# The state space model's two tables of powers, multiplied out on GpSimd instead of VectorE

## The chip, the core and the metric

The kernel runs on one core of a Trainium2 chip. The core has a matrix engine (TensorE, in the profile PE, with its weight loads as PEld), VectorE (DVE), ScalarE (ACT), GpSimd (POOL) and SyncE (SP), which issues most DMAs. Each engine works through its own queue of instructions in order; semaphores tie the queues together. The metric is the device time of one execution in microseconds; lower is better.

## What is computed

Three transformer-like blocks on 512 positions of width 1024, in float32. The first block mixes positions by four branches that are gated and merged: a linear-attention recurrence, a spatial gating unit, a short convolution and a diagonal state space model (S5). A feed-forward layer follows, then two attention layers with convolved feed-forward layers. The change touches the S5 branch:

```python
def s5_mixer(u, a_re, a_im, b_re, b_im, c_re, c_im, d, log_dt, glu_w):
    ...
    bb_re = q_re[..., None] * b_re - q_im[..., None] * b_im
    bb_im = q_re[..., None] * b_im + q_im[..., None] * b_re
    bu_re = jnp.einsum('gnc,bsgc->bsgn', bb_re, ug)
    bu_im = jnp.einsum('gnc,bsgc->bsgn', bb_im, ug)
    ...
    _, _, x_re, x_im = lax.associative_scan(_complex_affine_combine, (ar, ai, bu_re, bu_im), axis=1)
    y = (jnp.einsum('gcn,bsgn->bsgc', c_re, x_re) - jnp.einsum('gcn,bsgn->bsgc', c_im, x_im))
```

## The kernel before

Matrix products run in a split precision: `wload` (L142) fetches a weight tile of 128x1024 by a DMA on SP into `raw` (4 buffers), ScalarE rounds it to `whi` (L152) and VectorE subtracts to get `wlo` (L153, both 3 buffers); `mm3` (L169) then multiplies three times, hi by hi, hi by lo and lo by hi. So each weight tile costs VectorE one subtraction of 128x1024, and a matmul that reads `wlo` waits for it.

`_first_block` (L1165) writes its branches in this order: projections of the recurrence (`_rwkv`), the small parameters of S5 (`_s5_setup`, L950), the convolution (`_conv_branch`, products `cg` and `cy`), the spatial gating (`_sg_branch`, L878), the merge of the convolution (`_merge`, tiles `gp` and `yp`), the shift of the recurrence (`_rwkv_shift`, with dot products on VectorE, L328), the tables of S5 (`_s5_tables`, L1003) and its branch (`_s5_branch`). The program's scheduler doesn't keep this order. It takes for each engine the ready instruction that was written first, by its own idea of durations, and so fills gaps of one branch with instructions of a later one. The queue of each engine is fixed when the kernel is built.

In the gating, four value tiles `svp` are multiplied on TensorE, pass a GELU (`gelu2`, L243), are normalised on VectorE (`sgz`, L909 to L917) and go back to TensorE as weights of `sgm` (L928).

S5 works on chunks of eight positions. Its tables are two complex arrays of 128x(8 groups x 8 powers x 16 channels): Q holds powers 0 to 7 of the transition times the input matrix `bb`, W2 holds powers 1 to 8 times the output matrix `c4`. `_cmul` (L939) makes each from six operations of 128x1024, two for each of the four products and sums that make up the real and the imaginary part:

```python
    V.tensor_tensor(ore, are, bre, OP.mult)
    V.tensor_tensor(t, aim, bim, OP.mult)
    V.tensor_tensor(ore, ore, t, add)
    V.tensor_tensor(oim, aim, bre, OP.mult)
    V.tensor_tensor(t, are, bim, OP.mult)
    V.tensor_tensor(oim, oim, t, OP.subtract if conj else OP.add)
```

In the profile these are L942 to L947 with the tiles `s_Q`, `s_W` and the temporary `s_tq`; L1017 changes the sign of the imaginary part of W2. TensorE transposes Q (`s5q`, L1031) and multiplies it with `cb`, the output matrix (`s5k`, L1037, 32 small matmuls). ScalarE copies that product to `s_kt`; a DMA of POOL's queue takes it to a scratch in HBM, twelve more bring it back spread out as `s_ti` (L1048), and VectorE copies it into the Toeplitz tiles `s_toe` (L1051). `s5y` (L1138, L1141) multiplies W2 and `s_toe` near the end of the branch. Beside these, VectorE makes a table of rotations `s_ph` by doubling (L1056 to L1076, again by `_cmul`, on small tiles).

Of the kernel before, what the change touches and what calls it, by code (L numbers as in the profile page):

```python
# [18 lines left out]
OP = mybir.AluOpType  # L19
# [919 lines left out]
def _cmul(V, ore, oim, are, aim, bre, bim, t, conj=False):  # L939

    add, sub = (OP.add, OP.subtract) if conj else (OP.subtract, OP.add)
# [6 lines that stand above are left out]
# [55 lines left out]
def _s5_tables(K, sp, z):  # L1003
    nc, V = K.nc, K.nc.vector
    pr, pi, bb, c4, mag, sn, cs, s = (z[n] for n in ("pr", "pi", "bb", "c4", "mag", "sn", "cs", "s"))
    t8 = lambda n: sp.tile([128, 8], F32, name=n)

    Q = [K.g(f"s5_Q{x}", "e4", shape=(128, 8, 128)) for x in range(2)]
    W2 = [K.g(f"s5_W{x}", "e4", shape=(128, 8, 128)) for x in range(2)]
    tq = K.g("s5_tq", "e4", shape=(128, 8, 128))  # L1010
    v4 = lambda z: z.rearrange("p g (k c) -> p g k c", k=8)
    w = [128, 8, 8, 16]
    pk = lambda z, o: z[:, :, o:o + 8].unsqueeze(3).to_broadcast(w)
    mk = lambda z: z.unsqueeze(2).to_broadcast(w)
    _cmul(V, v4(Q[0]), v4(Q[1]), pk(pr, 0), pk(pi, 0), mk(bb[:, 0]), mk(bb[:, 1]), v4(tq))
    _cmul(V, v4(W2[0]), v4(W2[1]), pk(pr, 1), pk(pi, 1), mk(c4[:, 0]), mk(c4[:, 1]), v4(tq))
    V.tensor_scalar(W2[1], W2[1], -1.0, None, OP.mult)  # L1017

    cb = K.g("s5_cb", "e", shape=(128, 2, 8, 32))
    nc.gpsimd.memset(cb, 0.0)  # L1020
    for h in range(2):
        hs = slice(h * 64, (h + 1) * 64)
        V.tensor_copy(cb[hs, 0, :, h * 16:(h + 1) * 16], c4[hs, 0])
        V.tensor_scalar(cb[hs, 1, :, h * 16:(h + 1) * 16], c4[hs, 1], -1.0, None, OP.mult)

    QT = [K.g(f"s5_QT{x}", "e4", shape=(128, 8, 128)) for x in range(2)]
    for x in range(2):
        for q4 in range(2):
            ps = K.sm("s5q")
            for p in range(4):  # L1030
                nc.tensor.transpose(ps[:, p * 128:(p + 1) * 128], Q[x][:, 4 * q4 + p], K.ident)  # L1031
            nc.scalar.copy(QT[x][:, 4 * q4:4 * q4 + 4].rearrange("p a b -> p (a b)"), ps)

    ps = K.sm("s5k")
    for p in range(8):
        for x in range(2):
            nc.tensor.matmul(ps[:, p * 32:(p + 1) * 32], lhsT=Q[x][:, p], rhs=cb[:, x, p], start=x == 0, stop=x == 1)  # L1037
    kt = sp.tile([128, 256], F32, name="s5_kt")
    nc.scalar.copy(kt, ps[:, 0:256])
    scr = K.scratch.tile([128, 256], F32, name="s5_scr")  # L1040
    nc.gpsimd.dma_start(scr, kt)
    ti = [K.g(f"s5_ti{x}", "e4", shape=(128, 4, 256)) for x in range(2)]
    toe = [K.g(f"s5_toe{x}", "e4", shape=(128, 8, 128)) for x in range(2)]
    for x in range(2):
        nc.gpsimd.memset(ti[x], 0.0)
        for j in range(4 * x + 4):
            i0, o = max(j - 4 * x, 0), (7 - j) * 16
            nc.gpsimd.dma_start(ti[x][o:o + 16, i0:4],  # L1048
                                scr.rearrange("(k c) f -> c k f", c=16)[:, 4 * x + i0 - j:4 * x + 4 - j])
        for y in range(2):  # L1050
            V.tensor_copy(toe[y].rearrange("p g (i c) -> p g i c", i=8)[:, :, 4 * x:4 * x + 4],  # L1051
                          ti[x][:, :, y * 128:(y + 1) * 128].rearrange("p i (g c) -> p g i c", g=8))

    t2 = t8("s5_t2")
    for _ in range(3):
        V.tensor_tensor(mag, mag, mag, OP.mult)  # L1056
        V.tensor_tensor(t2, sn, cs, OP.mult)
        V.tensor_tensor(s, sn, sn, OP.mult)
        V.tensor_scalar(sn, t2, 2.0, None, OP.mult)
        V.tensor_scalar(cs, s, -2.0, 1.0, OP.mult, OP.add)  # L1060
    ph = [K.g(f"s5_ph{x}", "e", shape=(128, 8, 64)) for x in range(2)]
    tp = sp.tile([128, 8, 32], F32, name="s5_tp")
    V.memset(ph[0][:, :, 0:1], 1.0)
    V.memset(ph[1][:, :, 0:1], 0.0)
    V.tensor_copy(ph[0][:, :, 1], cs)
    V.tensor_copy(ph[1][:, :, 1], sn)
    n = 1
    while n < 63:
        m = min(n, 63 - n)
        last = lambda z: ph[z][:, :, n:n + 1].to_broadcast([128, 8, m])  # L1070
        _cmul(V, ph[0][:, :, n + 1:n + m + 1], ph[1][:, :, n + 1:n + m + 1], ph[0][:, :, 1:m + 1],
              ph[1][:, :, 1:m + 1], last(0), last(1), tp[:, :, 0:m])
        n += m
    rr = K.g("s5_rr", "e", shape=(128, 8, 64))
    V.tensor_copy(rr, mag.unsqueeze(2).to_broadcast([128, 8, 64]))
    V.memset(rr[:, :, 0:1], 0.0)  # L1076
    return dict(W2=W2, toe=toe, QT=QT, ph=ph, rr=rr)
# [87 lines left out]
def _first_block(K):  # L1165
    nc, d = K.nc, K.dram
    with ExitStack() as mix:
# [5 lines left out]
        with K.tags(e=9, e4=8):  # L1173
            with K.tc.tile_pool(name="s5", bufs=1) as sp:
                x, g1, rs = _start(K)
                tiles = _rwkv(K, x, g1, rs)
                last = K.last
                with K.tc.issue_after(K.split_1):
                    z = _s5_setup(K, sp)
                yc = _conv_branch(K)  # L1180
                yb = _sg_branch(K, last)
                acc = [K.g(f"acc{m}", "xr") for m in range(8)]
                for _ in _merge(K, 2, yc, acc, ada):
                    pass
                la, pairs = _rwkv_shift(K, tiles, rs)
                with K.tc.issue_after(last):
                    tab = _s5_tables(K, sp, z)
            yd = _s5_branch(K, tab)
# [482 lines left out]
```

## Time and profile before

| | |
|---|---|
| Median of three runs | 2148.33 us (2146.29 to 2150.67) |
| Profiled execution | 2149.2 us |
| Its span, first to last instruction | 2147.4 us |
| PE, PEld busy | 98%, 79% |
| DVE busy | 66% |
| ACT busy | 43% |
| POOL busy | 1% |
| Granted clock of TensorE, mean | 0.992 |

The rows below come from one profiled execution. A busy share is of the whole span. In a timeline a row gives the start, the busy time, the engine, the line, the operation with its output and inputs, the shapes and the count; idle time before it and what ended it stand in brackets. Successive operations of one engine overlap, so they start closer together than their busy time. The granted clock is the share of its full rate (2.4 GHz) that TensorE was given; half of it is 1.2 GHz.

### The profile page before, as it was taken

The page shows a single profiled execution, that of the slowest core. Times are in us where ns is not written, and L with a number is a line of the kernel's source. Part 1 is how long each engine was busy: PE and PEld are TensorE (multiplying, and loading weights), DVE is VectorE, ACT ScalarE, POOL GpSimd, SP SyncE. Part 2 cuts the span into 40 slices and gives each one's busy share as a digit, 9 for nine tenths or more (in the row PEclk, how much of TensorE's full clock was granted, in tenths as well). Part 3 has the DMA queues.
Part 4 walks back from the last instruction along what each step waited for, and adds up shares of the span by engine and source line. Part 5 has one row for each costly group of instructions (what it writes and reads, how often), then busy time and mean ns, then how long its engine had stood idle before and what let it go on. Part 6 is the DMA issues. An engine that isn't in the chain of part 4 may idle for free.

```text
span 2147.4 us, 29518 instructions
## 1 busy us (share of the span) xinstructions
PE 2094.6 (98%) x11502; PEld 1692.7 (79%) x11502; DVE 1416.1 (66%) x2655; ACT 934.1 (43%) x1549; POOL 23.5 (1%) x44
## 2 busy tenths in 40 slices
PE   6999999999999999999999999999999999999998
PEld 4877787888888888897778888888887778788887
DVE  7997884755734344558876756747568867575775
ACT  3334432333523232446764423324469944243433
POOL 0010000000000000000000000000000000000000
PEclk9999999999999999999999999999999999999999
DMA  8355441123322232232212222232321122323222
GB/s 329 106 182 180 159 148 50 60 84 133 108 98 89 98 98 89 99 119 89 80 50 98 98 93 94 89 98 81 128 79 40 60 79 86 101 83 105 97 81 67
DMA packets 68091, 220.47 MB, mean 103 GB/s; under 512 B 8068, under 2 KB 11060, under 8 KB 67952
## 3 DMA queue, kind: packets, MB, share of 16 engines
q1 hardware_dynamic: 64704, 210.19, 29.6%
q0 software_dynamic: 2096, 6.30, 1.0%
q8 instruction: 91, 1.49, 0.3%
q10 hardware_dynamic: 1152, 2.10, 0.3%
q14 instruction: 48, 0.39, 0.1%
HBM read 215.25 MB, written 3.30 MB: 102 GB/s over the span
## 4 chain that ended last, share of the span: by engine, by line
PE 85%; DVE 6%; ACT 4%; DMA 2%; issue 1%; DVEq 0%; ACTq 0%; SPq 0%
PE mm L174 62%; PE gp L174 7%; PE vt L174 3%; PE yp L174 2%; DMA raw<-ada_w 2%; PE pT L1336 1%; DVE wlo L153 1%; PE po L1349 1%; PE fin L174 1%; PE s L1316 1%; PE s L1317 1%; ACT whi L152 1%; DVE raw L328 1%; ACT p L1324 1%; PE pmt L643 1%
## 5 line engine op out<-in xcount | busy, mean ns | idle before, releaser
L174 PE MATMUL mm<-hi,whi 128*128 128x512 f32 x2088 | 829.7, 398 | 19.1 <-ACT hi L161 17.8
L174 PE MATMUL mm<-hi,wlo 128*128 128x512 f32 x2088 | 830.5, 398 | 1.1 <-DVE wlo L153 1.1
L174 PE MATMUL mm<-lo,whi 128*128 128x512 f32 x2088 | 829.2, 397 | 1.1 <-DVE lo L165 0.5
L152 ACT ACTIVATE whi<-raw 128x1024 fp32r<-128x1024 f32 (+3 forms) x341 | 350.3, 1030 | 754.9 <-PE mm L174 600.9
L153 DVE TENSOR_TENSOR wlo<-raw,whi 128x1024 fp32r<-128x1024 f32 (+3 forms) x341 | 403.5, 1186 | 180.2 <-ACT whi L152 170.7
L174 PEld LDWEIGHTS mm<-hi,whi 128*128 128x128 f32 x2088 | 395.7, 190 | 110.3 <-ACT hi L161 20.8
L174 PEld LDWEIGHTS mm<-lo,whi 128*128 128x128 f32 x2088 | 394.9, 189 | 91.1 <-DVE lo L165 2.7
L174 PEld LDWEIGHTS mm<-hi,wlo 128*128 128x128 f32 x2088 | 394.7, 189 | 89.9 <-DVE wlo L153 2.0
L1521 DVE TENSOR_TENSOR u<-mm,spr 128x512 f32<-128x512 f32 x88 | 60.6, 688 | 82.5 <-PE mm L174 82.2
L174 PE MATMUL gp<-hi,wlo 128*128 128x512 f32 x256 | 102.7, 401 | 3.3 <-DVE wlo L153 3.3
L174 PE MATMUL gp<-hi,whi 128*128 128x512 f32 x256 | 104.1, 407 | 0.9 <-ACT whi L152 0.9
L174 PE MATMUL gp<-lo,whi 128*128 128x512 f32 x256 | 102.9, 402 | 0.0
L1541 DVE TENSOR_TENSOR x<-x,mm 128x512 f32<-128x512 f32 x48 | 33.0, 687 | 96.1 <-PE mm L174 96.1
L1240 DVE SCALAR_TENSOR_TENSOR x<-mm,modv,x 128x512 f32<-128x512 f32 x32 | 24.0, 751 | 91.0 <-PE mm L174 91.0
L1522 ACT ACTIVATE cv<-u,vecs 128x512 f32<-128x512 f32 x88 | 71.3, 810 | 3.4 <-DVE u L1521 3.2
L1524 DVE SCALAR_TENSOR_TENSOR cv<-u,vecs,cv 128x510 f32<-128x510 f32 x88 | 66.0, 750 | 3.1
L1523 DVE SCALAR_TENSOR_TENSOR cv<-u,vecs,cv 128x511 f32<-128x511 f32 x88 | 65.6, 746 | 2.3 <-ACT cv L1522 2.1
L1532 ACT ACTIVATE cth<-cv 128x512 f32<-128x512 f32 x44 | 27.8, 632 | 86.2 <-DVE cv L1524 86.2
L174 PEld LDWEIGHTS gp<-hi,wlo 128*128 128x128 f32 x256 | 48.4, 189 | 15.6 <-DVE wlo L153 5.1
L1324 ACT ACTIVATE p<-p,at_m 128x128 f32<-128x128 f32 (+1 forms) x96 | 53.4, 557 | 14.7 <-DVE at_m L1323 13.7
L174 PEld LDWEIGHTS gp<-hi,whi 128*128 128x128 f32 x256 | 48.6, 190 | 13.4 <-ACT whi L152 1.8
L174 PEld LDWEIGHTS gp<-lo,whi 128*128 128x128 f32 x256 | 48.6, 190 | 10.6 <-issue 0.4
(532 smaller groups left out, 2612.1 us busy)
## 6 DMA issues: line engine op xcount, KB each, us to landing
raw<-w_up SPq DMA_DIRECT2D x88, 512.0 KB, 3.3
raw<-ffn_w SPq DMA_DIRECT2D x64, 512.0 KB, 3.3
raw<-w_in SPq DMA_DIRECT2D x49, 512.0 KB, 3.4
raw<-ada_w SPq DMA_DIRECT2D x32, 512.0 KB, 3.9
raw<-w_down SPq DMA_DIRECT2D x32, 384.0 KB, 3.1
ada_w<-ada_w SPq DMA_DIRECT2D x16, 512.0 KB, 8.7
raw<-w_out SPq DMA_DIRECT2D x16, 512.0 KB, 3.4
raw<-w_down SPq DMA_DIRECT2D x16, 512.0 KB, 3.3
```

Of the source, the lines that this page charges most:

```text
L152: nc.scalar.activation(hi[:, :n], raw[:, :n], AF.Copy)
L153: nc.vector.tensor_tensor(lo[:, :n], raw[:, :n], hi[:, :n].bitcast(F32), OP.subtract)
L174: self.nc.tensor.matmul(out, lhsT=a, rhs=b, start=first and n == 0, stop=last and n == total - 1)
L328: K.nc.vector.tensor_tensor_reduce(raw, raw, row, scale, 0.0, OP.mult, OP.add, out)
L1240: V.scalar_tensor_tensor(K.xr[m], ps, K.modv[:, 40 + m:41 + m], K.xr[m], OP.mult, OP.add)
L1324: A.activation(p[:, 0:n], p[:, 0:n], AF.Exp, bias=nm, scale=-1.0, accum_out=l)
L1521: V.tensor_tensor(u, ps, rs, OP.mult)
L1522: A.activation(c, u, AF.Identity, bias=K.vec("conv_b_2", l * 44 + j), scale=tap(2))
L1523: V.scalar_tensor_tensor(c[:, 1:], u[:, 0:S - 1], tap(1), c[:, 1:], OP.mult, OP.add)
L1524: V.scalar_tensor_tensor(c[:, 2:], u[:, 0:S - 2], tap(0), c[:, 2:], OP.mult, OP.add)
L1532: A.activation(th, gt, AF.Tanh, scale=0.5)
L1541: V.tensor_tensor(K.xr[m], K.xr[m], ps, OP.add)
```

## The change

The two complex products that make Q and W2, and the sign change of W2, are issued on GpSimd in place of VectorE. The operations, their operands and the tiles are the same.

```diff
     pk = lambda z, o: z[:, :, o:o + 8].unsqueeze(3).to_broadcast(w)
     mk = lambda z: z.unsqueeze(2).to_broadcast(w)
-    _cmul(V, v4(Q[0]), v4(Q[1]), pk(pr, 0), pk(pi, 0), mk(bb[:, 0]), mk(bb[:, 1]), v4(tq))
-    _cmul(V, v4(W2[0]), v4(W2[1]), pk(pr, 1), pk(pi, 1), mk(c4[:, 0]), mk(c4[:, 1]), v4(tq))
-    V.tensor_scalar(W2[1], W2[1], -1.0, None, OP.mult)
+    G = nc.gpsimd
+    _cmul(G, v4(Q[0]), v4(Q[1]), pk(pr, 0), pk(pi, 0), mk(bb[:, 0]), mk(bb[:, 1]), v4(tq))
+    _cmul(G, v4(W2[0]), v4(W2[1]), pk(pr, 1), pk(pi, 1), mk(c4[:, 0]), mk(c4[:, 1]), v4(tq))
+    G.tensor_scalar(W2[1], W2[1], -1.0, None, OP.mult)
```

Lines behind the diff are one higher in the changed kernel (L1037 becomes L1038). The scheduler makes other queues of it, up to the middle of the recurrence; from there on all queues are the same.

VectorE's queue, where the first table product stood; the numbers in the names tell buffers apart (`wlo_889` is the split that the first `svp` reads). Before:

```order
L870 SCALAR_TENSOR_TENSOR cy_789<-cg_659,vecs_69,cy_789 128x510
L942 TENSOR_TENSOR s5_Q0_1674<-s5_pw_609,s5_bb_651 128x1024
L943 TENSOR_TENSOR s5_tq_1678<-s5_pw_609,s5_bb_651 128x1024
L863 TENSOR_TENSOR cg_724<-mm_763,cg_724 128x512
L153 TENSOR_TENSOR wlo_889<-raw_887,whi_888 128x1024
L870 SCALAR_TENSOR_TENSOR cy_829<-cg_724,vecs_69,cy_829 128x511
L944 TENSOR_TENSOR s5_Q0_1674<-s5_Q0_1674,s5_tq_1678 128x1024
```

The same place in the changed kernel, the last rows ahead of `wlo_889`:

```order
L1077 MEMSET s5_rr_1826 128x8
L1060 TENSOR_SCALAR s5_sn_539<-s5_t2_1767 128x8
L1061 TENSOR_SCALAR s5_xr_540<-s5_s_636 128x8
L1067 COPY s5_ph1_1784<-s5_sn_539 128x8
L1066 COPY s5_ph0_1783<-s5_xr_540 128x8
L863 TENSOR_TENSOR cg_724<-mm_763,cg_724 128x512
L942 TENSOR_TENSOR s5_ph0_1783<-s5_ph0_1783 128x8
L943 TENSOR_TENSOR s5_tp_1785<-s5_ph1_1784 128x8
L153 TENSOR_TENSOR wlo_889<-raw_887,whi_888 128x1024
L870 SCALAR_TENSOR_TENSOR cy_829<-cg_724,vecs_69,cy_829 128x511
```

The table products are gone from the queue, and the small operations of the rotation tables, 18 of them (beside `cg`) up to `wlo_889`, have come forward.

POOL's queue in the changed kernel, from the memset of `cb` on (before, the memset of `ti0` came next):

```order
L1021 MEMSET s5_cb_1692 128x512
L942 ISA
L942 TENSOR_TENSOR s5_Q0_1674<-s5_pw_609,s5_bb_651 128x1024
L943 TENSOR_TENSOR s5_tq_1678<-s5_pw_609,s5_bb_651 128x1024
L945 TENSOR_TENSOR s5_Q1_1675<-s5_pw_609,s5_bb_651 128x1024
L944 TENSOR_TENSOR s5_Q0_1674<-s5_Q0_1674,s5_tq_1678 128x1024
L942 TENSOR_TENSOR s5_W0_1676<-s5_pw_609,s5_bc_533 128x1024
L946 TENSOR_TENSOR s5_tq_1678<-s5_pw_609,s5_bb_651 128x1024
L945 TENSOR_TENSOR s5_W1_1677<-s5_pw_609,s5_bc_533 128x1024
L947 TENSOR_TENSOR s5_Q1_1675<-s5_Q1_1675,s5_tq_1678 128x1024
```

Q0 is complete with the fourth product and Q1 with the eighth. The other four products, the sign change, the memset of `ti0` and the DMAs of `kt` and `ti` follow.

TensorE's queue at the `s5k` of the tables and the `sgm` of the gating. Before:

```order
L1037 MATMUL s5k<-s_cb,s_Q_1674 128x32
L1037 MATMUL s5k<-s_cb,s_Q_1675 128x32
L928 MATMUL sgm<-sg_wsT,sgz 64x128 x4
L174 MATMUL mm<-hi,whi 128x512
L174 MATMUL mm<-lo,whi 128x512
```

And now:

```order
L1038 MATMUL s5k<-s_cb,s_Q_1675 128x32
L1038 MATMUL s5k<-s_cb,s_Q_1674 128x32
L928 MATMUL sgm<-sg_wsT,sgz 64x128 x2
L174 MATMUL mm<-hi,whi 128x512
L928 MATMUL sgm<-sg_wsT,sgz 64x128 x2
L174 MATMUL mm<-lo,whi 128x512
```

Before, all 32 `s5k` stood ahead of `sgm`; now 19 do, and of the other 13 the last four stand ahead of the S5 projection.

## Rows read from the trace of the kernel before

**Rows 1.** The page's first part: TensorE's busy time, its share, instructions.

```profile
PE 2094.6 (98%) x11502; PEld 1692.7 (79%) x11502; DVE 1416.1 (66%) x2655; ACT 934.1 (43%) x1549; POOL 23.5 (1%) x44
```

**Rows 2.** Busy time of each engine by stretch.

```profile
core 0: us, PE busy (x) PEld busy (x) DVE busy (x) ACT busy (x) POOL busy (x), PEclk, DMA share, GB/s
85.00:119.60 34.60, 34.60 (x206) 30.48 (x205) 34.10 (x63) 13.81 (x25) 0.00 (x0) 1.00 0.34 115
125.00:130.00 5.00, 1.57 (x12) 1.32 (x12) 5.00 (x19) 0.37 (x1) 0.76 (x2) 0.50 0.48 167
```

**Rows 3.** Timeline of TensorE, 100 to 137 us.

```profile
100.81 0.28 PE L174 MATMUL svp<-wlo,hi 128*128 128x256 f32 x1
...
119.57 2.18 PE L1031 MATMUL s5q<-k_ident,s_Q 128*128 128x128 f32 x16
121.66 4.12 PE L1037 MATMUL s5k<-s_cb,s_Q 128*128 128x32 f32 x32
129.21 1.12 PE L928 MATMUL sgm<-sg_wsT,sgz 128*64 128x128 f32 x8 [3.43 <-DVE sgz L917]
...
136.22 0.39 PE L174 MATMUL mm<-hi,whi 128*128 128x512 f32 x1
```

**Rows 4.** Timeline of VectorE, 88 to 130 us.

```profile
88.11 0.28 DVE L947 TENSOR_TENSOR s_bb<-s_bb,s_tb 128x128 f32<-128x128 f32 x1
...
88.97 1.22 DVE L942 TENSOR_TENSOR s_Q<-s_pw,s_bb 128x1024 f32<-128x1024 f32 x1
90.10 1.22 DVE L943 TENSOR_TENSOR s_tq<-s_pw,s_bb 128x1024 f32<-128x1024 f32 x1
91.24 0.68 DVE L863 TENSOR_TENSOR cg<-mm,cg 128x512 f32<-128x512 f32 x1
91.84 1.22 DVE L153 TENSOR_TENSOR wlo<-raw,whi 128x1024 fp32r<-128x1024 f32 x1
...
113.14 0.42 DVE L909 BATCH_NORM_STATS2 bn_s<-sgz 128x6 f32<-128x256 f32 x1
...
126.29 1.21 DVE L947 TENSOR_TENSOR s_W<-s_W,s_tq 128x1024 f32<-128x1024 f32 x1
...
129.48 0.68 DVE L1017 TENSOR_SCALAR s_W<-s_W 128x1024 f32<-128x1024 f32 x1
```

**Rows 5.** Timelines of VectorE and TensorE around the wait at 171 us.

```profile
154.51 0.42 DVE L1051 COPY s_toe<-s_ti 128x512 f32<-128x512 f32 x1
...
169.94 1.22 DVE L153 TENSOR_TENSOR wlo<-raw,whi 128x1024 fp32r<-128x1024 f32 x1
...
171.21 0.50 PE L174 MATMUL gp<-hi,wlo 128*128 128x512 f32 x1 [2.05 <-DVE wlo L153]
...
173.19 0.63 PE L174 MATMUL gp<-hi,whi 128*128 128x512 f32 x1
```

**Rows 6.** Timeline of VectorE: the last of the rotation tables' operations.

```profile
173.40 0.42 DVE L947 TENSOR_TENSOR s_ph<-s_ph,s_tp 128x248 f32<-128x248 f32 x1
```

**Rows 7.** Timeline of POOL.

```profile
54.14 0.96 POOL L1045 MEMSET s_ti<- 128x1024 f32 x1 [50.61 <-DVE modv L328]
...
129.78 2.26 POOL L1048 DMA_DIRECT2D s_ti<-s_scr  x4 [2.75 <-DMA s_scr<-s_kt]
132.04 0.97 POOL L1045 MEMSET s_ti<- 128x1024 f32 x1
133.30 4.13 POOL L1048 DMA_DIRECT2D s_ti<-s_scr  x8 [0.29 <-POOL s_ti L1045]
```

**Rows 8.** Timeline of VectorE beside the two memsets of POOL.

```profile
54.69 2.07 DVE L407 SCALAR_TENSOR_TENSOR x<-x,g,spr 128x512 f32<-128x512 f32 x3
...
131.71 1.33 DVE L1059 TENSOR_SCALAR s_sn<-s_t 128x8 f32<-128x8 f32 x1
```

**Rows 9.** Timelines of ScalarE and TensorE: the S5 projection's copy, the Toeplitz tiles' reader.

```profile
206.09 0.57 ACT L1085 COPY s5u<-mm 128x512 f32<-128x512 f32 x1
...
232.47 0.56 PE L1141 MATMUL s5y<-s_ub,s_toe 128*128 128x64 f32 x4
```

## The prediction

> **What bounds the kernel now.** The page's first part says that TensorE is busy for 98% of the span [rows 1], so work on another engine costs time only where TensorE waits for it. The stretch table comes next. Between 85 and 119.6 us TensorE never pauses, but VectorE is busy for 34.10 of 34.60 us; right behind, TensorE works for 1.57 us of five, at a granted clock of 0.50, which is 1.2 of its 2.4 GHz [rows 2]. The timeline of TensorE shows why. It does the transposes `s5q` (119.57) and the products `s5k` (from 121.66), both read from the table Q, and then idles 3.43 us before `sgm` at 129.21, released by VectorE's normalised `sgz` (L917). At 136.22 matmuls are back at 0.39 us [rows 3]. So for some 6.7 us after the wait it ran at half clock, which costs about half of that, 3.3 us: **6.7 us** for the wait and its clock. VectorE was late because its queue was full: the twelve table products, from 88.97 us on, stand among the weight splits (`wlo`) and the gating arithmetic [rows 4]. A second wait of 2.05 us, on a `wlo` at 169.94, comes from the same full queue; seven matmuls behind it take 0.63 in place of 0.39 us, 1.7 us more [rows 5]. Together **10.4 us** of TensorE's time hang on VectorE's queue between 89 and 171 us.
>
> **The change, part by part.**
>
> *Removed from VectorE.* Twelve products start 1.13 us apart (88.97 to 90.10), 13.6 us; the sign change of W2[1] holds the queue for about 0.6 (busy 0.68) [rows 4]: 14.2 us. The four `toe` copies leave the stretch too, as their input now comes later: 4 x 0.42 = 1.7 busy [rows 5], some 1.4 by start to start. The last two small products of the phase table come in ahead of the wait at 171 (0.7). VectorE's queue up to 171 us is **14.9 us** shorter.
>
> *Moved on VectorE.* 52 small operations of the rotation tables (`s_ph`, `s_rr` and their sources) stand ahead of the gating arithmetic now instead of between 130 and 173.4 us. The last and longest is busy for 0.42 us [rows 6], most for 0.2 and overlapping: some 7 us, and no new work. But 18 of them, beside `cg`, now precede the `wlo` of 91.84 that the first `svp` needs at 100.81; it had ended by 93.06, so that split has 7.7 us of cover [rows 3, 4].
>
> *Added on POOL.* Thirteen instructions of 128x1024. No two-input operation of POOL is in this trace. The nearest row is its memset of the same size: 0.96 us for one stream [rows 7]. A product reads two streams and writes one. Side by side they give 0.96, one after another 2.88; I take two, **1.92 us**, since the write can overlap the reads. Twelve of those and 0.96 for the sign change are **24.0 us** (12.5 to 35.5). POOL can start when the table `s_bb` is done, 88.4 us [rows 4]. The transposes need Q1, the eighth product: 88.4 + 8 x 1.92 = 103.8, at the dear end 111.4, both ahead of 119.57 [rows 3]. If POOL runs freely, Q is in time, with at least 8 us of cover. By the Trainium skill (GPSIMD Engine Reference, section 3.1), which gives 4497 ns for 2048 elements, one product would be an estimated 2.25 us and POOL's work about 28 us.
>
> *Who else waits on POOL.* Behind the tables in POOL's queue stand the memset of `ti`, the DMA of `kt` and twelve of `ti`. They wait for `s5k` anyway, of which 13 of 32 now stand behind `sgm`, the last four just ahead of the projection whose copy `s5u` starts at 206.09 [rows 9]. From there: 2.75 us for the DMA of `kt`, 6.4 to issue the twelve others, 1 for the memset [rows 7], so about 214 with landing. The reader is `s5y` at 232.47 [rows 9]: hidden, with 18 us of cover. W2 is read by the same `s5y`. SP swaps a few neighbouring loads; TensorE gets no new work. I cost these at nothing.
>
> *Do the two engines run side by side?* This decides the sign. When POOL's memset ran at 132.04, a VectorE operation on 128x8 elements took 1.33 us from 131.71 and ended as the memset did; at 54.14 three operations with two inputs passed beside another memset undisturbed, 0.69 us each [rows 7, 8]. So the engines do hold each other off, for a whole instruction, but not in every combination. The pair that matters, two SBUF inputs on VectorE against a POOL instruction that reads, is not in this trace. Nothing lost is one bound; the other is all of POOL's 24.0 us, less what VectorE can do meanwhile with one input or one in PSUM: three operations of 0.68 (`cg` and two `cy`) and two of 0.42 (`bn_stats`), 2.9 us [rows 4]. That is 21.1 us. I take the upper end, since the row that shows a hold shows a full one, and most of VectorE's work here has two inputs in SBUF. The Trainium skill (SBUF — State Buffer, section "Who interferes with whom") says just this of that pair, an exclusive lock for the whole instruction, and that a GpSimd instruction that only writes spares two-input ones. Both memset rows agree with it; no row here shows the reading pair.
>
> *The sum.* VectorE's queue at 171 us: -14.9 + 21.1 = +6.2 us. TensorE waits for it there as before, and the waits move forward: the first is at `svp` (100.81), where the 18 small operations ahead of its split face POOL's, and the clock falls again there instead of at 129. The wait at `sgm` goes, but what is late next is the `wlo` stream. The profiled execution took 2149.2 us, 0.87 above the median of the runs, 2148.33. So 2149.2 + 6.2 = 2155.4, and against the median **2154.5 us**.
>
> **The rivals.**
>
> *Side by side, so faster.* The two engines barely hold each other, and VectorE's queue is 14.9 us shorter. TensorE reaches `sgm` after 19 of the 32 `s5k` at about 124 [rows 3]; VectorE, which before came to `sgz` behind all twelve products, is done by then. This gives back 6.7 us, with the wait at 171 up to 10.4: 2141.6 to 2137.9, say 2140. For it: DMA issues of POOL beside VectorE's work, and the pass at 54 us. Against: the hold at 131.71. It decides where VectorE loses less than 14.9 us, that is, under some six tenths of POOL's work.
>
> *POOL is the one held off, so no change.* If VectorE's back-to-back queue keeps the port, POOL advances only in its gaps. Up to 119.57 VectorE is freed of eleven products, all but that at 126.29 [rows 4], 12.4 us, takes in about 7 of small table work, and has 2.9 that hold nothing: 8.3 us for the 15.4 that Q needs. TensorE then waits 7.1 us at `s5q` in place of 3.43 at `sgm`: +3.7, less the 3.75 of the second wait, which the shorter queue removes. That is 2148.3. For it: VectorE is busy 34.10 of 34.60 us [rows 2]. Against: at 131.71 it was VectorE that was held.
>
> *A dearer POOL, so slower still.* At 2.88 us a product, 35.5 - 2.9 - 14.9 = +17.7: 2166.
>
> *The products don't move.* The order shows them on POOL, so this rival is out.
>
> **How the numbers follow.** A measurement of this kernel can tell about 0.2% (4.3 us) from no change. I give the forecast, with its dearer form, 0.52; faster 0.35; held-off POOL 0.13. Of the forecast's cases a few land within 0.2%, since 21.1 is an upper end for that price of POOL. So faster 0.35, same 0.17, slower 0.48. The range must reach the faster rival and the dear end: **2138.5 to 2166**, which leaves out about 0.1 on either side. The forecast's own range is 2149 to 2166.
>
> **What would show it.** Right: POOL's products at about 2 us or more, `wlo` (L153) longer than its 1.13 between 89 and 120 us or tiny VectorE operations of 1 to 2 us there, a wait of TensorE before or in `svp`, no wait at `sgm`. Wrong: `wlo` unchanged, TensorE without a pause from 85 to 165 us (faster), or a wait at `s5q` released by POOL (no change).

## The result, and the profile after

The changed kernel takes **2169.09 us** (median of four runs, 2164.95 to 2171.54) against 2149.5 us for the kernel before in the same comparison: ratio 1.0092, 95% interval 1.0075 to 1.0110. It is slower by 0.9%, and 3 us above the upper end of the predicted range. The profiled execution took 2164.95 us with a span of 2163.2 us, 15.8 more than before.

The page's first part answers to [rows 1]:

```profile
PE 2092.3 (97%) x11502; PEld 1689.3 (78%) x11502; DVE 1425.6 (66%) x2642; ACT 933.3 (43%) x1549; POOL 54.7 (3%) x57
```

VectorE is no less busy than before (1425.6 against 1416.1 us), although twelve products and a sign change have left it. POOL took on 31 us. Busy time by stretch, to be set against [rows 2]:

```profile
core 0: us, PE busy (x) PEld busy (x) DVE busy (x) ACT busy (x) POOL busy (x), PEclk, DMA share, GB/s
85.00:100.00 15.00, 14.51 (x63) 11.44 (x61) 15.00 (x15) 1.06 (x1) 14.17 (x7) 1.00 0.10 35
100.00:105.00 5.00, 0.00 (x0) 0.00 (x0) 4.99 (x7) 0.00 (x0) 4.92 (x3) 0.67 0.00 0
105.00:110.00 5.00, 1.18 (x4) 0.91 (x5) 5.00 (x6) 1.67 (x2) 4.84 (x3) 0.50 0.00 0
110.00:115.00 5.00, 2.09 (x10) 1.79 (x9) 5.00 (x5) 0.00 (x0) 4.83 (x3) 0.50 0.31 105
115.00:120.00 5.00, 1.40 (x6) 1.40 (x7) 4.83 (x21) 1.42 (x2) 3.17 (x2) 0.50 0.01 2
120.00:125.00 5.00, 2.29 (x14) 2.00 (x13) 4.90 (x15) 0.79 (x2) 0.00 (x0) 0.78 0.35 108
125.00:130.00 5.00, 5.00 (x31) 5.00 (x30) 3.44 (x8) 0.66 (x2) 0.00 (x0) 0.66 0.64 192
...
240.00:260.00 20.00, 17.01 (x103) 14.83 (x102) 17.07 (x28) 2.32 (x4) 0.00 (x0) 0.91 0.29 95
```

Where TensorE hardly paused before (24.95 us of work from 100 to 125), it now works 6.96 of these 25 us, mostly at a granted clock of 0.50. From 100 to 115 us VectorE passes five to seven operations in five microseconds, POOL three. The timeline of TensorE names the waits; the last row is the same `gp` in the part where all queues are alike:

```profile
106.40 0.55 PE L174 MATMUL svp<-whi,hi 128*128 128x256 f32 x1 [6.89 <-DVE cg L863]
109.37 0.58 PE L174 MATMUL svp<-wlo,hi 128*128 128x256 f32 x1 [2.42 <-DVE wlo L153]
...
118.60 0.58 PE L174 MATMUL svp<-whi,hi 128*128 128x256 f32 x1 [6.51 <-DVE cy L872]
...
124.23 0.39 PE L174 MATMUL svp<-whi,hi 128*128 128x256 f32 x1 [2.71 <-DVE cy L872]
...
145.38 0.44 PE L928 MATMUL sgm<-sg_wsT,sgz 128*64 128x128 f32 x4 [0.35 <-DVE sgz L917]
...
249.00 0.80 PE L174 MATMUL gp<-hi,wlo 128*128 128x512 f32 x1 [2.99 <-DVE wlo L153]
...
383.08 0.50 PE L174 MATMUL gp<-hi,whi 128*128 128x512 f32 x1 [0.91 <-ACT whi L152]
```

The same matmul in the kernel before:

```profile
364.71 0.50 PE L174 MATMUL gp<-hi,whi 128*128 128x512 f32 x1 [0.91 <-ACT whi L152]
```

By then the changed kernel is 18.4 us behind. It had come to its first wait at `svp` 1.2 us ahead (at 99.51; the kernel before starts `svp` at 100.69), so the stretch between the two costs 19.6 us. Most of it adds up. Waits at `svp`: 6.89 + 2.42 + 6.51 + 2.71 = 18.5. Work at a lowered clock, busy time by what is missing from 1.00 in the rows from 105 to 130: 0.59 + 1.05 + 0.70 + 0.50 + 1.70 = 4.5. A new wait at 249.00 with its lowered clock: 2.99 + 17.01 x 0.09 = 4.5. Given back: the wait at `sgm` with its clock, 6.7 [rows 3], and about 2.8 of the 3.75 around 171 us [rows 5], of which a wait of 0.94 stays. 18.5 + 4.5 + 4.5 - 9.5 = 18.0. Behind this matmul, where the queues are the same, the profiled execution took 2.6 us less than that of the kernel before. So its span shows 15.8 us more (19.6 - 1.2 - 2.6); it is the fastest of the four, and the medians differ by 19.6.

POOL and VectorE in the same stretch:

```profile
84.80 3.16 POOL L942 TENSOR_TENSOR s_Q<-s_pw,s_bb 128x1024 f32<-128x1024 f32 x1 [81.24 <-DVE s_bb L944]
...
91.13 1.94 POOL L945 TENSOR_TENSOR s_Q<-s_pw,s_bb 128x1024 f32<-128x1024 f32 x1
93.03 2.41 POOL L944 TENSOR_TENSOR s_Q<-s_Q,s_tq 128x1024 f32<-128x1024 f32 x1
95.40 1.95 POOL L942 TENSOR_TENSOR s_W<-s_pw,s_bc 128x1024 f32<-128x1024 f32 x1
...
101.28 2.34 POOL L947 TENSOR_TENSOR s_Q<-s_Q,s_tq 128x1024 f32<-128x1024 f32 x1
...
113.95 3.32 POOL L1018 TENSOR_SCALAR s_W<-s_W 128x1024 f32<-128x1024 f32 x1
```

```profile
84.74 1.21 DVE L153 TENSOR_TENSOR wlo<-raw,whi 128x1024 fp32r<-128x1024 f32 x1
...
91.19 1.91 DVE L1057 TENSOR_TENSOR s_mag<-s_mag 128x8 f32<-128x8 f32 x1
93.02 0.15 DVE L1058 TENSOR_TENSOR s_t<-s_sn,s_xr 128x8 f32<-128x8 f32 x1
93.10 2.37 DVE L1059 TENSOR_TENSOR s_s<-s_sn 128x8 f32<-128x8 f32 x1
...
105.58 0.68 DVE L863 TENSOR_TENSOR cg<-mm,cg 128x512 f32<-128x512 f32 x1
...
108.11 1.21 DVE L153 TENSOR_TENSOR wlo<-raw,whi 128x1024 fp32r<-128x1024 f32 x1
109.24 2.42 DVE L870 SCALAR_TENSOR_TENSOR cy<-cg,vecs,cy 128x511 f32<-128x511 f32 x1
...
117.86 0.68 DVE L872 TENSOR_TENSOR cy<-mm,cy 128x512 f32<-128x512 f32 x1
```

An operation on 128x8 elements lasts as long as the product on POOL beside it (1.91 beside 1.94, 2.37 beside 2.41), the next one passes in 0.15, and then it is POOL's turn again. `cg`, with one input in PSUM (the memory that takes TensorE's results), passes in its usual 0.68. But it stands behind these small operations: it starts at 105.58 instead of 91.24, the second `wlo` at 108.11 instead of 91.84, the first `cy` of L872 at 117.86 instead of 96.57. That `cy` in the kernel before:

```profile
96.57 0.68 DVE L872 TENSOR_TENSOR cy<-mm,cy 128x512 f32<-128x512 f32 x1
```

### The profile page after: what moved, and what is told of

It is laid out like the page before. It is cut to its first block, busy times and chain, and to the rows that moved or that the text cites. A ratio compares the mean times of both kernels' runs of the same rounds, so it can differ in the third digit from the quotient of the medians.

```text
span 2163.2 us, 29524 instructions
## 1 busy us (share of the span) xinstructions
PE 2092.3 (97%) x11502; PEld 1689.3 (78%) x11502; DVE 1425.6 (66%) x2642; ACT 933.3 (43%) x1549; POOL 54.7 (3%) x57
## 4 chain that ended last, share of the span: by engine, by line
PE 86%; DVE 7%; ACT 4%; DMA 1%; issue 1%; POOL 0%; DVEq 0%; ACTq 0%; POOLq 0%
PE mm L174 62%; PE gp L174 8%; PE vt L174 3%; PE yp L174 2%; PE pT L1337 1%; PE po L1350 1%; DVE wlo L153 1%; PE fin L174 1%; PE s L1317 1%; PE s L1318 1%; ACT whi L152 1%; DMA raw<-ada_w 1%; ACT p L1325 1%; PE pu L637 1%; PE pmt L643 0%
## 5 line engine op out<-in xcount | busy, mean ns | idle before, releaser
L1337 PE MATMUL pT<-k_ident,p 128*128 128x128 f32 x304 | 53.9, 279 | 3.0 <-ACT p L1334 2.4
```

What stands on the lines that cost most here:

```text
L1337: T.transpose(pp[:, b * 128:(b + 1) * 128], p[:, b * 128:(b + 1) * 128], K.ident)
```

## The experiments

Two theories were on trial. **Turns**: a product on POOL holds VectorE for its whole length, the two take turns, and TensorE pays since `cg`, `wlo` and `cy` stand behind the turns. **Order**: the new queue of VectorE alone costs it. Each run stands against the kernel before on the same chip.

| Run | Median, us | Ratio to the kernel before (95%) |
|---|---|---|
| no products | 2149.03 | 0.9996 (0.9985 to 1.0007) |
| no products, one dot held | 2144.74 | 0.9985 (0.9974 to 0.9995) |
| writes only on POOL | 2153.17 | 1.0027 (1.0005 to 1.0049) |
| products in halves | 2171.21 | 1.0103 (1.0088 to 1.0118) |
| rotations later | 2154.40 | 1.0027 (1.0016 to 1.0039) |
| only W2 on POOL | 2158.34 | 1.0039 (1.0024 to 1.0054) |
| four PSUM buffers | 2168.68 | 1.0091 (1.0073 to 1.0109) |
| all on POOL, late | 2168.56 | 1.0083 (1.0068 to 1.0098) |
| Q on POOL, W2 late on VectorE | 2152.26 | 1.0011 (1.0000 to 1.0022) |
| all late on VectorE | 2149.90 | 0.9996 (0.9985 to 1.0008) |
| W2 late on VectorE | 2146.90 | 0.9977 (0.9967 to 0.9987) |
| W2 later still | 2146.31 | 0.9981 (0.9971 to 0.9991) |

### Port or order: the products left out

```diff
-    _cmul(G, v4(Q[0]), ...)
-    _cmul(G, v4(W2[0]), ...)
-    G.tensor_scalar(W2[1], W2[1], -1.0, None, OP.mult)
+    for z in (*Q, *W2):
+        G.memset(z, 0.0)
```

> The changed kernel without the twelve products and the sign change: Q and W2 are filled with zeros by four early writes on GpSimd, so the tables' values are left out. The queue of VectorE in the stretch of the loss, with 18 small operations ahead of the first cg and wlo, is that of the changed kernel. If GpSimd's products hold VectorE (the port), the waits of 6.89, 2.42, 6.51 and 2.71 us at svp are gone, cg (L863) runs near 91 us, and the time is 2138 to 2142. If the new order of VectorE's queue is what costs, the waits at svp stay for the most part and the time is above 2158.

VectorE's operations come in the same order as in the changed kernel, from the `wlo` of 84.74 up to 380 us there, so the products on POOL are the difference, and every wait at `svp` is gone. VectorE's timeline, for the rows above:

```profile
84.20 1.23 DVE L153 TENSOR_TENSOR wlo<-raw,whi 128x1024 fp32r<-128x1024 f32 x1
...
88.74 0.68 DVE L863 TENSOR_TENSOR cg<-mm,cg 128x512 f32<-128x512 f32 x1
...
89.52 1.22 DVE L153 TENSOR_TENSOR wlo<-raw,whi 128x1024 fp32r<-128x1024 f32 x1
...
94.63 0.68 DVE L872 TENSOR_TENSOR cy<-mm,cy 128x512 f32<-128x512 f32 x1
```

From the first `wlo` to `cy` it is 10.43 us here and 33.12 with POOL's products (84.74 to 117.86): the products hold VectorE for **22.7 us**. Order alone falls. Yet the time is 2149.0, not the 2138 to 2142 that the 10.4 us of the prediction and this expectation gave: with this queue, taking 14.2 us off VectorE is worth nothing that can be measured (0.9985 to 1.0007). TensorE's timeline shows where the gain went, the second row being the wait that stood at 171 us:

```profile
122.06 0.44 PE L928 MATMUL sgm<-sg_wsT,sgz 128*64 128x128 f32 x4 [0.35 <-DVE sgz L917]
...
162.88 0.50 PE L174 MATMUL gp<-hi,wlo 128*128 128x512 f32 x1 [1.37 <-DVE wlo L153]
...
228.56 0.80 PE L174 MATMUL gp<-hi,wlo 128*128 128x512 f32 x1 [4.68 <-DVE wlo L153]
```

The third is new, and the changed kernel has it too (2.99 at 249.00). VectorE's timeline ahead of it:

```profile
216.01 1.23 DVE L328 CUSTOM_DVE_ANT_0 raw<-raw,c_row 128x1024 f32<-128x1024 f32 x1 [4.21 <-DMA raw<-ada_w]
...
217.16 0.69 DVE L942 TENSOR_TENSOR s_z<-s_b,s_ph 128x512 f32<-128x512 f32 x1
...
227.28 1.23 DVE L153 TENSOR_TENSOR wlo<-raw,whi 128x1024 fp32r<-128x1024 f32 x1
```

In the new queue a dot product that waits 4.21 us for its DMA stands ahead of the chain of S5's scan, and that chain ahead of the `wlo`. The wait and the lowered clock around it (34.62 us of work at 0.91 from 200 to 240 us, 3.1 us) take back 7.8 of the 9.1 us that the two old waits give (6.7 at `sgm`, 2.4 of the 3.75 around 171 us); a new wait of 1.25 us at `s5q` for ScalarE takes the rest.

### The dot product held back

On top of the run without products (`K.z_done` is set behind the last chain of `s_z`):

```diff
-        _dot(K, ..., 0.5, after)
+        _dot(K, ..., 0.5, K.z_done if j == 32 else after)
```

> The run without the products (tables' values left out) with one more edit: one dot product of the modulation vector (L328), which stood ahead of the scan of S5 and waited 4.21 us for its DMA at 211.6, is held behind the last chain of s_z, and with it the wlo that TensorE waited 4.68 us for at 228.6 comes ahead of the scan. If the place of that dot in VectorE's queue is what took back the gain of the shorter queue, the wait of 4.68 us and its half clock go: 2139 to 2144 against 2149.0 without the edit. If the gain was lost elsewhere, or another wlo becomes late in its place: 2146 to 2151.

The wait of 4.68 us is gone, and the stretch from 200 to 240 us has 38.75 us of TensorE work at full clock in place of 34.62 at 0.91. By the ratios that gives back 0.11%, some 2.4 us, by the medians 4.3; the two intervals overlap, so the gain isn't clear of noise, and 2144.74 is just above the range that I had set. The two profiles agree with a gain: from the first `svp` to the `gp` that the kernel before starts at 364.71 it is 261.3 us here and 264.7 without the edit. In its place stand smaller waits (1.64 at `s5q` for ScalarE, 1.94 at `pu`, L638). So the place of that dot probably took part of the gain; where the rest goes stays open.

### Shorter turns

```diff
-    _cmul(G, v4(Q[0]), v4(Q[1]), pk(pr, 0), ...)
+    for h in (0, 4):
+        _cmul(G, hv(Q[0]), hv(Q[1]), ph_(pr, 0), ...)
```

(`hv` and `ph_` take four of the eight powers; the same for W2.)

> Every product on GpSimd in two halves of 128x512 (24 instructions of about 1 us in place of 12 of 2); the work and VectorE's queue up to the gating are the same. If the two engines take turns by whole instructions, one small operation of VectorE waits about 1 us in place of 1.9, cg (L863) is done by about 97 us in place of 106, TensorE's first wait at svp falls from 6.89 us to under 2, the later two at cy shrink too, and the time is 2150 to 2160 (the changed kernel: 2169). If it is the sum of GpSimd's work that counts, or the order, or the lateness of Q, nothing changes or it gets worse by the start of 12 more instructions: 2168 to 2174.

The first half came true and the second didn't. `cg` starts at 100.23, small operations wait about 1 us (1.04, 1.05, 1.26), and the first wait shrinks to 2.03. Then:

```profile
119.75 0.58 PE L174 MATMUL svp<-whi,hi 128*128 128x256 f32 x1 [14.11 <-DVE cy L872]
```

The `cy` of L872 stands behind some twenty more rotation operations, and VectorE passed only one or two per turn until POOL's last product was done, at 117.7 us. From the first `wlo` to that `cy` VectorE took 32.5 us, and 33.1 in the changed kernel: it waited about twice as often, for half as long each time. The time lies in the range of the sum of GpSimd's work, not in that of turns: as long as VectorE has small operations enough to meet every turn, POOL's time is what counts.

### Fewer operations that face the turns

```diff
+    with K.tc.issue_after(K.sg_normed):
-    t2 = t8("s5_t2")
+        t2 = t8("s5_t2")
...
```

(All of the rotation tables stand in the block.)

> The changed kernel, but the rotation tables (all behind t2) are issued on VectorE behind the normalisation of the gating, so that cg, wlo and cy face GpSimd's products alone. If it is the turns by whole instructions, cg comes at about 90, the first svp in time, but each of the following two-input operations (wlo, cy L870, lo) waits a product of about 2 us: some 13 turns of 2 us against 15 us that VectorE's queue lost, so TensorE still waits some microseconds in the svp or before sgm: 2146 to 2158. If the order alone is what costs, the time falls below the kernel before, to 2138 to 2142. If neither, it stays at 2165 to 2172.

With the small operations behind the gating, `cg` starts at 90.81, and each turn of POOL is matched by work that is needed anyway:

```profile
91.41 2.37 DVE L153 TENSOR_TENSOR wlo<-raw,whi 128x1024 fp32r<-128x1024 f32 x1
93.70 5.24 DVE L870 SCALAR_TENSOR_TENSOR cy<-cg,vecs,cy 128x511 f32<-128x511 f32 x2
```

Some 14 of the 20 us are gone (1.0027 in place of 1.0092). The rest stays as waits of 3.83 at `svp` for `cy`, 3.34 for ScalarE's GELU (`gl_s`), itself behind VectorE, and 2.29 at `sgm`. So the loss is turns times order: order alone costs nothing (no products), and the same thirteen instructions cost 5.4 us here (2154.40 less 2149.03) in place of 20.

Only W2 on POOL:

```diff
-    _cmul(G, v4(Q[0]), ...)
+    _cmul(V, v4(Q[0]), ...)
```

> Only W2's six products and its sign change go to GpSimd; Q stays on VectorE, where its products stand among cg, wlo and cy as in the kernel before, and the small rotation operations come only after the second wlo. If the loss is turns of whole instructions times the number of VectorE's operations ahead of cg and cy, seven turns of some 2.2 us (15 us, from about 86 to 104 us) meet long operations that are needed anyway: cg before 96 us, the waits at svp together under 6 us, 2150 to 2158. If each instruction on GpSimd costs the same wherever it falls, 7/13 of the 20 us by which the changed kernel stands above the one without products: 2157 to 2163.

2158.34: 0.3 us above the one forecast and inside the other, so it doesn't tell them apart. `cg` came at 92.84 and only 1.82 us was lost at `svp`, as turns have it. But W2's third product waited until 103.08 for the temporary `s_tq` that Q used on VectorE, and then the turns held VectorE's operations ahead of its part of the GELU: `lo` took 2.87 us and `wlo` 2.96, `gl_s` (L250) came at 118.65, and TensorE waited 8.80 for ScalarE's `gl_s` at 121.46.

### What holds: reading or writing

```diff
-    _cmul(G, ...)
+    G.tensor_copy(gate, bb[:, 0, 0, 0:1])
+    for o in (Q[0], tq, Q[1], ...):
+        G.memset(o, 0.0)
+        G.memset(o, 0.0)
```

> In place of the products GpSimd issues 25 memsets of 128x1024 on the same tiles, behind one small operation that reads s_bb: about as long on GpSimd as the products (25 x 0.96 = 24 us from about 85 us on), but nothing is read; the tables' values are left out. If what holds VectorE is an instruction of GpSimd that reads, operations of VectorE with two inputs pass beside the memsets and only copies and scalar operations of one input are held, by up to 0.96 us each (of the 18 small ones ahead of wlo about 9 have one input): cg by about 98 us, time 2139 to 2150. If any busy GpSimd holds VectorE alike, cg comes near 100 us and later, two-input operations are stretched to 1 us too, and the time is 2152 to 2162. If the order is what costs, above 2158.

Eight of its ten runs took 2148.94 to 2155.53 us and two 2166.05 and 2169.1; the profile is that of the longest, so it shows a case that occurs and not the usual one. VectorE's timeline there, POOL's memsets running from 87.61 to 109.14 us without a gap:

```profile
88.40 0.76 DVE L870 SCALAR_TENSOR_TENSOR cy<-cg,vecs,cy 128x510 f32<-128x510 f32 x1
89.06 20.10 DVE L1065 TENSOR_SCALAR s_sn<-s_t 128x8 f32<-128x8 f32 x1
89.14 20.04 DVE L1066 TENSOR_SCALAR s_xr<-s_s 128x8 f32<-128x8 f32 x1
89.21 19.97 DVE L1062 TENSOR_TENSOR s_mag<-s_mag 128x8 f32<-128x8 f32 x1
```

A `cy` with two inputs passes beside a memset in its usual time (0.76 us). The scalar operation with one input behind it did not get one turn in 20 us; it ended at 109.16, in the first gap between two memsets (109.14 to 109.20). The two rows under it, the last with two inputs, stand behind it in the queue and end with it, so they don't show a hold of their own. Reading is thus not the only thing that holds; which operation is held depends on both sides. The median lies in the second range, of a GpSimd that holds everything alike, but the rows speak against that reading, and the first range had not allowed for a hold of this length. The run leaves open why.

### The link to TensorE

```diff
-        tags(space=PSUM, mm=3, sm=5)
+        tags(space=PSUM, mm=4, sm=4)
```

> The changed kernel with four PSUM buffers for mm in place of three, and four in place of five for sm, in the first block. If svp waits for cg and cy since these free the PSUM buffers that svp needs, the wait of 6.89 us for cg goes, and svp waits next for the wlo behind it in the same queue of VectorE, some 2 us later than cg; of the two later waits for cy (6.51 and 2.71) the last goes or moves: 2160 to 2169. If the buffers are not the link, the waits for cg and cy stay as they are: 2167 to 2172. The products' turns with VectorE stay in both cases, so it can't come near the kernel before.

```profile
108.80 0.58 PE L174 MATMUL svp<-wlo,hi 128*128 128x256 f32 x1 [9.78 <-DVE wlo L153]
...
118.07 0.58 PE L174 MATMUL svp<-whi,hi 128*128 128x256 f32 x1 [3.99 <-DVE cy L872]
...
123.71 0.58 PE L174 MATMUL svp<-whi,hi 128*128 128x256 f32 x1 [2.71 <-DVE cy L872]
```

The wait for `cg` is gone and the `wlo` behind it takes its place, 9.78 against 6.89 + 2.42. So `svp` waited for a PSUM buffer that `cg` had to free, and would have waited for the `wlo` next anyway: the time doesn't move. (It lies where the two forecasts overlap, so the rows decide and not the time.) Of the waits for `cy` the first shrank to 3.99 and the last, which I had thought would go, stayed at 2.71.

### Another place, another engine

All thirteen instructions on POOL, behind the first merged tile `acc0`:

```diff
+    G.tensor_copy(gate, K.acc0[:, 0:1])
+    with K.tc.issue_after(nc.cur_bb.bb.instructions[-1]):
...
```

> The changed kernel with all thirteen instructions on GpSimd held until acc0 is done (about 171 us), by one small copy of a column of acc0. They then meet VectorE's wlo, rkv and modv operations in a stretch where VectorE is only 58 per cent busy and none of the rotation operations is left. If the loss is turns of whole instructions ahead of what TensorE waits for, wlo there is held by about 2 us each, with few operations ahead of it: 2146 to 2156, svp without a wait. If GpSimd's sum of about 28 us costs the same anywhere: 2165 to 2172.

`acc0` is done at 144 us, earlier than the 171 that I wrote, so POOL's work ran from 144.74 to 180.4. The whole came out as slow as the changed kernel, though no rotation operation stood in POOL's way. Its fair measure is the run with the same work late on VectorE (below), which has the same pause ahead of `sgm` (4.58 here, 4.49 there): against its 2149.90 POOL costs 18.7 us. TensorE's waits:

```profile
170.13 0.77 PE L174 MATMUL gp<-hi,whi 128*128 128x512 f32 x1 [6.09 <-DVE acc L848]
...
180.41 0.80 PE L174 MATMUL gp<-hi,wlo 128*128 128x512 f32 x1 [7.80 <-DVE wlo L153]
```

VectorE's timeline:

```profile
172.09 2.40 DVE L328 CUSTOM_DVE_ANT_0 w_t<-w_t,sh_row 128x512 f32<-128x512 f32 x1
...
174.43 3.35 DVE L328 CUSTOM_DVE_ANT_0 raw<-raw,c_row 128x1024 f32<-128x1024 f32 x1
```

Dot products of 0.69 and 1.23 us took 2.40 and 3.35, with `wlo` and `acc` behind them. Between 130 and 175 us TensorE needs a `wlo` every 7 us or so, and VectorE was nearly full there before as well (9.93, 9.54 and 8.72 us of ten from 130 on, 14.08 of 15 from 160). My range for turns (2146 to 2156) failed: it rested on the idle time behind 175 us, which only the last 5 us of the work reached. A further pause of 3.43 us ahead of `z` (L519, 278.44) has no releaser in the trace; the changed kernel waits 0.46 us there for VectorE's `lora_s`, and why it is longer here stays open.

Q alone on POOL, W2 on VectorE behind `acc0`, the rotation tables behind the gating:

> Only Q's six products on GpSimd; W2's stay on VectorE but behind acc0, and the rotation tables behind the gating's normalisation, so that the six turns on GpSimd meet only operations that TensorE waits for anyway. If the loss is turns ahead of cg, wlo and cy: six turns of some 2.5 us against the 14 us that VectorE's queue ahead of sgm is shorter, so 2143 to 2151, above the kernel with only W2 late (2146.9) by 0 to 4 us. If GpSimd costs 1.5 us of TensorE per instruction anywhere: 2152 to 2158.

2152.26: 1.3 us above the range for turns, at the lower end of the second. One wait of 3.18 at `svp` for `cy` is left. Against the next run, which has Q on VectorE and the rotation tables where the scheduler puts them, it is 0.34% slower (1.0011 against 0.9977), some 7 us for six products.

No product on POOL, W2 moved within VectorE's queue:

```diff
+            if m == 0:
+                K.late = nc.cur_bb.bb.instructions[-1]
...
-    _cmul(V, v4(W2[0]), ...)
+    with K.tc.issue_after(K.late):
+        _cmul(V, v4(W2[0]), ...)
```

> The kernel before with W2's products and sign change still on VectorE, but issued behind the first merged tile acc0 (about 171 us), where VectorE is busy for 14.54 of 25 us (175 to 200); GpSimd does nothing new. If relieving VectorE's queue ahead of sgm is worth what the prediction took for it, the 3.43 us at sgm with its half clock and most of the 2.05 us at 171 go: 2138 to 2143. If a new order behind 200 us takes it back, as without any products (a wait of 4.68 us for a wlo at 228.6 that the kernel before does not have), 2146 to 2152.

0.9977: this version **beats both kernels**. W2 ran from 146.7 to 172.5 us, the wait at `sgm` is gone and the one at `gp` is 1.22. The gain of 0.23% (about 5 us, 3.4 by the medians) is at most half of the 10.4 that I had put on VectorE's queue. With `m == 3`:

> The run with only W2 late on VectorE, but W2's products behind the fourth merged tile (acc3, 166.5 us in that run) in place of the first (acc0, 144.8 us); TensorE's queue is the same. VectorE has more idle time from 175 us on (19.16 of 25 us busy in that run) than between 130 and 175. If what TensorE still loses there hangs on VectorE's queue (1.22 us for a wlo at 166.6), this wait goes: 2143 to 2146. If the remaining gain is used up, it stays at 2145 to 2149, as with acc0, and slower than that if W2's products now push the wlo behind 175 us.

0.9981, no different: W2 ran from 169.4 to 184, and the `wlo` at 167 still makes TensorE wait 1.63. Both complex products late on VectorE:

> The kernel before with all twelve products and the sign change on VectorE, but behind acc0 (about 171 us): 14.2 us of work into a stretch with some 10 us of idle VectorE. The transposes and s5k move behind it too, and the chain kt, scratch, ti, toe must end before s5y. If VectorE's queue up to sgm is what counted: 2138 to 2144. If the late chain or wlo behind the products becomes the next wait: 2146 to 2156, with waits at gp for wlo after 175 us or at s5y for s_toe.

0.9996, no gain. TensorE and VectorE ahead of `sgm`:

```profile
122.02 0.70 PE L930 MATMUL sgm<-sg_wsT,sgz 128*64 128x128 f32 x4 [4.49 <-issue]
```

```profile
121.51 0.75 DVE L919 TENSOR_TENSOR sgz<-sgz,sg_ln 128x256 f32<-128x256 f32 x2
```

The trace names no releaser ("issue"). But `sgm` starts 0.51 us behind the start of the last step of `sgz`, and 0.47 in the kernel before (128.74 and 129.21), so it is most likely the same wait. It is no shorter, since the transposes and `s5k` (2.18 and 4.12 us [rows 3]), which stood ahead of `sgm`, have moved behind it and no longer fill TensorE's time.

What POOL costs TensorE isn't one price for an instruction: 1.5 us each in the changed kernel (20.1 for thirteen), 1.4 late (18.7), 0.4 with the rotations later (5.4), about 1 for Q alone (5 to 7 for six, with the rotations later too). Turns as such stand in the rows of every run with products on POOL, but my ranges for them failed in the halves and in the late run, and narrowly with only W2 and with Q alone.

## Why the prediction was wrong

*The bound.* TensorE did wait on VectorE, and the waits at `sgm` and 171 us mostly went (0.35 and 0.94 stay in the changed kernel). But they were not worth 10.4 us: without any products the time stays (0.9996), as the queue that the scheduler makes then brings its next wait (4.68 us at 228.56). Behind 200 us I had priced `s5y` and `toe`, which held (no wait for them in the changed kernel), and not the place of `wlo`.

*The price on POOL.* I took 1.92 us from the memset for all twelve. The eight that multiply take 1.94 us where nothing stretches them (four rows), the four that add 2.34 to 2.41 (three rows). That makes some 25 us; the twelve take 28.2 in all, as POOL waits for its turns too. The sign change took 3.32 us and not 0.96. So POOL's work was 31.5 us in place of 24.0. The Trainium skill's figure (GPSIMD Engine Reference, section 3.1) is for an add, and its estimate of 2.25 us comes near the adds here; the multiplications are shorter.

*Side by side.* They are not, as forecast, and the signs that I had named came: tiny operations of 1.87 to 2.37 us, waits in `svp`, almost none at `sgm`. (Of the three operations beside the memset at 54.14 [rows 7, 8] only the first ran beside it, as it ended at 55.10; the run with writes only bears the reading out.) The Trainium skill (SBUF — State Buffer, section "Who interferes with whom") says that one engine fully blocks the other for a whole instruction; the rows agree (1.91 beside 1.94), and `cg`, with one input in PSUM, was spared at 0.68. The rival with a gain is out, the one that holds POOL off too: Q was in time, and no wait at `s5q` names POOL.

*The hold.* I put VectorE's loss at 21.1 us; it is 22.7. That it came so near is partly luck: I had taken POOL's work too short, and all of it but 2.9 us as held.

*The step that failed is the sum.* "-14.9 + 21.1 = +6.2 us" sets what leaves VectorE's queue against what holds it, as if TensorE only saw the balance at 171 us. It sees each at its own place. The 22.7 us all fall between 85 and 118 us, ahead of `cg`, `wlo` and `cy`, where the first `svp` had 7.7 us of cover; of the products removed, only two stood ahead of `cg` [rows 4]. What VectorE saves behind that point came too late for `svp`. It gave back 9.5 us at the two old waits, and the new queue's wait behind 200 us took about half of that again, 4.5. The term of 14.9 us was the one mis-sized: the run without products measures the removal, with its new queue, at nothing (0.9996), and the hold at 20.1 (2169.09 less 2149.03). Together that is +20 in place of +6.2.

*The small operations.* I had seen that 18 of them face POOL ahead of the first `svp`, and forecast that the waits move there. But I priced them by their length (0.2 us) and not by the turn that each pair of them costs. Eight were held ahead of `cg`, for 1.87 to 2.37 us each, 16.2 in all, and that uses up the cover of 7.7. Putting them later gave back some 14 us.

*The link.* I looked at the `wlo` of the first `svp` only. First to be missed was the PSUM buffer that `cg` frees, then two more by `cy`.

*The dearer POOL* (2166) came nearest, by accident: a product didn't take 2.88 us, and it was the sum that was short.

## What to carry to other kernels

Before work goes to GpSimd, look at what VectorE does meanwhile: while GpSimd's two-input operations run, count VectorE's operations ahead of the ones that TensorE waits for, and price each or each pair at a whole GpSimd instruction, however small it is, up to GpSimd's time in all. Don't net a hold against a saving on the same engine: each counts where the next consumer waits, and a saving that comes behind a wait doesn't shorten it. The cheaper move can be later in the same engine's queue, as W2 showed here.

## What was not expected of the hardware

While GpSimd's products ran, the two engines took turns by instructions: halving the products halved each hold (from about 1.9 to about 1.05 us) and changed nothing in the total. Against a stream of memsets VectorE did not get a turn at all, once: 20.10 us for an operation on 128x8 elements that takes 0.16 to 0.18 with GpSimd idle. Why the memsets gave no turn where the products did, and whether the eight shorter runs had such a hold, stays open.
